# An input projection in rounds of wide and then narrow matmuls, and a first unit written out by hand

## The chip, the core and the metric

The kernel runs on one core of one Trainium2 chip. The time is device time in microseconds, from the launch's first to its last work, as the median of several runs. Engines in the views: PE is TensorE's matmuls, PEld its weight loads, DVE is VectorE, ACT is ScalarE, POOL is GpSimd, SP is the engine that issues most transfers. L343 is line 343 of the kernel.

## What is computed

Two layers of a mixer over 256 frames of width 2048, all in float32. In each layer the normalised input goes through one combined projection of 9248 columns; a pooling branch and a scanned state-space branch make 4096 columns of it, which an output projection brings back to 2048:

```python
for layer in range(DEPTH):
    h = rms_norm(x, pre_norm_w[layer])
    proj = jnp.einsum('bld,de->ble', h, w_in[layer])
    ...
    y_pool = pool_mixer(pool_u, pool_mix_w[layer], pool_scale[layer]) * jax.nn.silu(pool_gate)
    y_ssd = ssd_branch(ssd_z, ssd_xbc, ssd_dt, conv_w[layer], conv_b[layer], ...)
    mixed = jnp.concatenate([y_pool.astype(x.dtype), y_ssd.astype(x.dtype)], axis=-1)
    out = jnp.einsum('ble,ed->bld', mixed, w_out[layer])
    x = x + rms_norm(out, post_norm_w[layer])
```

## The kernel before

**Split operands.** Every matrix product is made from float32 numbers that are split into a high and a low part (type float32r): high weight times high and low input, and low weight times high input. The input `hs` holds, for each of its 16 slices of 128 rows, 256 columns of high parts and behind them 256 of low parts. A *wide* matmul takes a high weight block of 128x128 (`wh`) over all 512 columns, a *narrow* one the low block (`wl`) over the first 256. Both add to the same accumulator (`acc[m]`, 512 columns); `halves_sum` later adds its two halves with a ScalarE copy and a VectorE add, at a priority of 200 instructions ahead (`P_EVAC`).

**Units and halves.** Weights come in units of 512 rows by 512 columns (`raw`, three buffers, one transfer each on SP's queue; the first two units in pieces). Each unit is split in two halves of 256 rows by `emit_split`: ScalarE writes `wh`, VectorE subtracts and writes `wl`, five buffers each (`NW`). `run_ahead` emits the splits up to five halves past the one in use, with a priority of 15 instructions ahead (`P_SPLIT`), and fills free raw buffers.

**Chunks.** `chunk` makes 512 output columns: four accumulators of 128 columns, all four of the pool, over 16 slices, that is four units or 64 wide and 64 narrow matmuls. A layer has 18 such chunks: B, C and, for each of four groups, x, z, u and gate; behind each gate chunk stands a mix chunk of one unit (`pl` in place of `hs`). The first and the last unit go accumulator by accumulator through both halves, the middle ones half by half; `mm_m` does, for one accumulator and one half, wide, narrow, wide, narrow. `mid` is called twice in a unit and lets the background generators (scan, time steps, parameter loads) emit their next step. Chunk C also has 32 matmuls for the time-step columns in front of its first two units (`dt_unit`).

**Planner.** The program is traced in this order; a planner then orders each engine's instructions by priority and expected readiness, places buffers and sets the waits. `behind(...)` and `high_priority` bind or move single instructions.

**Start.** The first input piece comes in three transfers on ScalarE's queue, the first weight unit in three on SP's, the norm weights (`pre_rows`) on POOL's. `keep_busy` gives TensorE filler matmuls on the identity: 11 before the transpose of the norm weights, then the transposes of the first input slice (`piece`). In layer 0 the first unit goes slice by slice (`mm_k`, `by_k`, `piece_rest`), with the later slices' transposes and splits between.

Of the kernel before, what the change touches and what calls it, by code (L numbers as in the profile page):

```python
# [8 lines left out]
F32 = mybir.dt.float32  # L9
# [5 lines left out]
P = 128  # L15
# [26 lines left out]
def hybrid_kernel(ctx: ExitStack, tc, x, pre_norm_w, w_in, pool_mix_w, pool_scale, conv_w, conv_b,  # L42
# [15 lines left out]
    def t8():  # L58
        return work.tile([P, 8, SEQ], F32, name="t8", tag="t8", bufs=2)
# [86 lines left out]
    def emit_first(kk):  # L146
        if kk == 0:
            halves[0] = (wts.tile([P, 2, CW], F32R, name="wh", tag="wh", bufs=NW),
                         wts.tile([P, 2, CW], F32R, name="wl", tag="wl", bufs=NW))
            stream["split"] = 1  # L150
        wh, wl = halves[0]
        r = raws[0][:, kk]
        hi = nc.scalar.activation(out=wh[:, kk], in_=r, func=AF.Copy)
        lo = nc.vector.tensor_tensor(out=wl[:, kk], in0=r, in1=wh[:, kk].bitcast(F32), op=ALU.subtract)
        stream["last"] = (hi, lo)
# [48 lines left out]
    pre_rows = const.tile([DEPTH * NK, P], F32, name="pre_rows")  # L204
    load_pieces(x_in, emit_raw)
# [3 lines left out]
    nc.gpsimd.dma_start(out=pre_rows, in_=pre_norm_w.rearrange("l (a p) -> (l a) p", p=P))  # L209
# [38 lines left out]
    with tc.high_priority():  # L248
        idle = aux()
        filler = keep_busy(idle, 11)  # L250
# [5 lines left out]
        filler = pre_t  # L256
# [82 lines left out]
    def mm_m(acc, m, half, mov, k0, first, last):  # L339
        wh, wl = half  # L340
        cs = slice(m * P, (m + 1) * P)
        for kk in range(2):
            nc.tensor.matmul(acc[m], wh[:, kk, cs], mov[:, k0 + kk, :],  # L343
                             start=first and kk == 0, stop=False, skip_group_check=True)
            stream["mm"] = nc.tensor.matmul(acc[m][:, 0:SEQ], wl[:, kk, cs], mov[:, k0 + kk, 0:SEQ],  # L345
                                            start=False, stop=last and kk == 1, skip_group_check=True)

    def mm_k(acc, m, half, mov, k0, kk):
        wh, wl = half
        cs = slice(m * P, (m + 1) * P)  # L350
        nc.tensor.matmul(acc[m], wh[:, kk, cs], mov[:, k0 + kk, :],
                         start=k0 + kk == 0, stop=False, skip_group_check=True)
        stream["mm"] = nc.tensor.matmul(acc[m][:, 0:SEQ], wl[:, kk, cs], mov[:, k0 + kk, 0:SEQ],
                                        start=False, stop=False, skip_group_check=True)

    def chunk(mov, nk, pre_unit=None, mid_unit=None, by_k=None):
# [8 lines left out]

        for q in range(nq):
            if pre_unit is not None:
                pre_unit(q)
            if q == 0 and by_k is not None:
                hf = [next_half(False)]  # L370
                for h in range(2):
                    for kk in range(2):
                        if kk == 0 and h == 1:
                            hf.append(next_half(False))
                        for m in range(4):
                            mm_k(acc, m, hf[h], mov, 2 * h, kk)
                        if kk == 0 and h == 0:
                            by_k()
                        if h == 1:
                            mid(q, kk)  # L380
# [231 lines left out]
    later_k = []  # L612

    def piece(c):
        pts = [None, None]
        if c > 0:
            transpose_piece(c, range(NT), pts)
            return split_piece(0, c, hs, pts)
        with behind(filler):
            turned = transpose_piece(0, range(NT), pts, range(1))  # L620
        emit_first(0)
        with behind(pre_copy, *stream["last"]):
            first = split_piece(0, 0, hs, pts, range(1))
        turned = keep_busy(idle, 2, turned)
        with behind(turned):
            turned = transpose_piece(0, range(NT), pts, range(1, 2))
        with behind(*first):
            emit_first(1)
        with behind(*stream["last"]):
            second = split_piece(0, 0, hs, pts, range(1, 2))  # L630
        later_k.append((pts, second))
        return second

    def piece_rest():
        pts, second = later_k.pop()
        with behind(stream["mm"]):
            transpose_piece(0, range(NT), pts, range(2, 4))
        with behind(*second):
            rest = split_piece(0, 0, hs, pts, range(2, 4))
        with behind(*rest):  # L640
            run_ahead(2)
        return rest
# [3 lines left out]
    for l in range(DEPTH):  # L646
# [3 lines left out]
        gate = {0: piece(0)}  # L650
# [27 lines left out]
        def first_k(gate=gate):  # L678
            gate[0] = piece_rest()

        acc = chunk(hs, NK, None, first_mid, first_k if l == 0 else None)
# [29 lines left out]
        for g in range(NG):  # L711
# [18 lines left out]
            pl = work.tile([P, 4, CW], F32R, name="pl", tag="t8", bufs=2)  # L730
# [18 lines left out]
        pwb = work.tile([P, D_MODEL], F32, name="pwb", tag="t8", bufs=2)  # L749
# [132 lines left out]
```

## Time and profile before

| | us |
|---|---|
| median of 3 runs | 1284.42 (1284.25 to 1284.48) |
| the profiled execution | 1283.68 |
| its span, from the first to the last instruction | 1282.0 |
| TensorE busy in it | 1268.5 |
| VectorE, ScalarE, GpSimd busy | 919.9, 707.7, 194.1 |

A group of instructions by line has their count, the time in which any of them ran, the mean length of one in ns, and the idle time of the engine in front of them with what ended it. Ends of matmuls are modelled, and one matmul starts while the one before drains; where the pace of TensorE matters, starts are compared and not lengths. A row of the timeline has the start, the time until the last of the merged instructions ends, engine, line, operation and tiles, and in brackets idle time of that engine ahead of it.

### The profile page before, as it was taken

Reading aid. Unit: us, or ns where it says so; the run is one execution under the profiler, and the core shown is the slowest. Engines: PE = TensorE matmul, PEld = TensorE weight load, DVE = VectorE, ACT = ScalarE, POOL = GpSimd, SP = SyncE. Lnnn points to the kernel's source line nnn. Section 1 sums busy time; section 2 is a strip of 40 time slices with the busy share of each in tenths; the row PEclk is TensorE's granted clock in tenths of the full one; section 3 lists DMA queues with packets and bytes.
Section 4 is the critical chain, followed back from the end, with each engine's and each line's share of the span. In section 5 each row is a group of like instructions: output and inputs, shape, how many; then the busy total and the mean of one; then the engine's idle time right before and its main releaser. Section 6 shows DMA issues by size and latency. Waiting matters only on the chain.

```text
span 1282.0 us, 17907 instructions
## 1 busy us (share of the span) xinstructions
PE 1268.5 (99%) x6988; PEld 1087.5 (85%) x6988; DVE 919.9 (72%) x1297; ACT 707.7 (55%) x893; POOL 194.1 (15%) x245
## 2 busy tenths in 40 slices
PE   8999999999999999999999999999999999999997
PEld 7888888888888888888878888888888888888886
DVE  5898778868778794444478978778788788844454
ACT  6656556566566574344375566566565665644442
POOL 0111211212213220000002121122112122200000
PEclk9999999999999999999999999999999999999999
DMA  8555566465474676555564655555654655856552
GB/s 277 199 198 198 164 205 204 151 229 166 163 246 149 209 273 203 190 190 189 186 211 164 219 177 169 203 187 170 223 198 139 222 189 173 295 197 198 192 189 79
DMA packets 127244, 249.47 MB, mean 195 GB/s; under 512 B 9304, under 2 KB 10392, under 8 KB 125880
## 3 DMA queue, kind: packets, MB, share of 16 engines
q1 hardware_dynamic: 124808, 237.25, 55.9%
q0 software_dynamic: 1536, 10.57, 2.3%
q8 instruction: 54, 0.88, 0.3%
q10 hardware_dynamic: 816, 0.52, 0.1%
q14 instruction: 30, 0.25, 0.1%
HBM read 244.06 MB, written 4.26 MB: 194 GB/s over the span
## 4 chain that ended last, share of the span: by engine, by line
PE 97%; ACT 2%; DVE 1%; issue 0%; POOL 0%; POOLq 0%; ACTq 0%
PE acc L343 43%; PE acc L345 22%; PE acc L768 9%; PE acc L767 9%; PE acc L769 9%; PE aux L551 1%; PE aux L556 1%; PE aux L704 1%; PE aux L517 1%; ACT t L314 1%; PE aux L297 0%; ACT wh L138 0%; PE aux L245 0%; ACT hs L306 0%; PE aux L576 0%
## 5 line engine op out<-in xcount | busy, mean ns | idle before, releaser
L343 PE MATMUL acc<-hs,wh 128*128 128x512 f32 x2288 | 809.0, 398 | 1.0 <-DVE hs L307 1.0
L139 DVE TENSOR_TENSOR wl<-raw,wh 128x1024 fp32r<-128x1024 f32 x431 | 535.7, 1252 | 252.4 <-ACT wh L138 252.2
L138 ACT ACTIVATE wh<-raw 128x1024 fp32r<-128x1024 f32 x431 | 451.1, 1058 | 415.5 <-PE acc L343 222.9
L345 PE MATMUL acc<-hs,wl 128*128 128x256 f32 x2288 | 639.6, 280 | 0.0
L343 PEld LDWEIGHTS acc<-hs,wh 128*128 128x128 f32 x2288 | 429.2, 188 | 102.1 <-DVE hs L307 1.5
L345 PEld LDWEIGHTS acc<-hs,wl 128*128 128x128 f32 x2288 | 431.6, 189 | 1.2 <-DVE wl L139 0.2
L407 POOL TENSOR_TENSOR t<-t,rb 128x256 f32<-128x256 f32 x144 | 140.0, 981 | 405.6 <-DVE t L401 377.6
L400 ACT COPY t<-acc 128x256 f32<-128x256 f32 x176 | 63.0, 366 | 69.1 <-PE acc L345 69.0
L767 PE MATMUL acc<-wh,pm 128*128 128x512 f32 x256 | 99.7, 389 | 0.0
L767 PE MATMUL acc<-wh,ms 128*128 128x512 f32 x256 | 99.6, 389 | 0.0
L769 PE MATMUL acc<-wh,ms 128*128 128x512 f32 x256 | 99.6, 389 | 0.0
L768 PE MATMUL acc<-wl,ms 128*128 128x512 f32 x256 | 99.6, 389 | 0.0
L769 PE MATMUL acc<-wh,pm 128*128 128x512 f32 x256 | 99.6, 389 | 0.0
L768 PE MATMUL acc<-wl,pm 128*128 128x512 f32 x256 | 99.6, 389 | 0.0
L401 DVE TENSOR_TENSOR t<-acc,t 128x256 f32<-128x256 f32 x176 | 71.4, 416 | 14.7 <-ACT t L400 13.9
L420 DVE SCALAR_TENSOR_TENSOR t<-t,cols,t 128x256 f32<-128x256 f32 x144 | 70.8, 521 | 0.1
L767 PEld LDWEIGHTS acc<-wh,ms 128*128 128x128 f32 x256 | 48.1, 188 | 10.1
L767 PEld LDWEIGHTS acc<-wh,pm 128*128 128x128 f32 x256 | 48.1, 188 | 10.0
L769 PEld LDWEIGHTS acc<-wh,pm 128*128 128x128 f32 x256 | 48.1, 188 | 10.0
L769 PEld LDWEIGHTS acc<-wh,ms 128*128 128x128 f32 x256 | 48.1, 188 | 10.0
L768 PEld LDWEIGHTS acc<-wl,ms 128*128 128x128 f32 x256 | 48.1, 188 | 9.9
L768 PEld LDWEIGHTS acc<-wl,pm 128*128 128x128 f32 x256 | 48.1, 188 | 9.8
(158 smaller groups left out, 845.4 us busy)
## 6 DMA issues: line engine op xcount, KB each, us to landing
raw<-in_w_in_dram SPq DMA_DIRECT2D x142, 1024.0 KB, 5.1
raw<-in_w_out_dram SPq DMA_DIRECT2D x64, 1024.0 KB, 5.2
t<-acs POOLq DMA_DIRECT2D x8, 1024.0 KB, 5.1
raw<-in_pool_mix_w_dram SPq DMA_DIRECT2D x8, 1024.0 KB, 5.4
t<-in_x_dram SPq DMA_DIRECT2D x7, 512.0 KB, 9.5
pwb<-in_post_norm_w_dram POOLq DMA_DIRECT2D x2, 1024.0 KB, 7.3
x_mid<-t SPq DMA_DIRECT2D x8, 256.0 KB, 2.9
t<-x_mid SPq DMA_DIRECT2D x4, 512.0 KB, 8.8
```

The lines of the kernel that those rows point to most:

```text
L138: hi = nc.scalar.activation(out=wh, in_=r, func=AF.Copy)
L139: lo = nc.vector.tensor_tensor(out=wl, in0=r, in1=wh.bitcast(F32), op=ALU.subtract)
L314: nc.scalar.activation(out=junk, in_=xp[c][:, T], func=AF.Square, accum_out=ssq[:, T, c:c + 1])
L343: nc.tensor.matmul(acc[m], wh[:, kk, cs], mov[:, k0 + kk, :], start=first and kk == 0, stop=False, skip_group_check=True)
L345: stream["mm"] = nc.tensor.matmul(acc[m][:, 0:SEQ], wl[:, kk, cs], mov[:, k0 + kk, 0:SEQ], start=False, stop=last and kk == 1, skip_group_ ...
L400: nc.scalar.copy(out=t[0:n], in_=acc[0:n, SEQ:CW])
L401: nc.vector.tensor_tensor(out=t[0:n], in0=acc[0:n, 0:SEQ], in1=t[0:n], op=ALU.add)
L407: nc.gpsimd.tensor_tensor(out=dest[:, m], in0=t, in1=rb, op=ALU.mult)
L420: nc.vector.scalar_tensor_tensor(out=dst[:, m], in0=pad[:, m, j:j + SEQ], scalar=cw[:, j, ct:ct + 1], in1=dst[:, m], op0=ALU.mult, op1=ALU ...
L767: nc.tensor.matmul(oacc[T], ah, wh[:, kk], start=first and kk == 0, stop=False)
L768: nc.tensor.matmul(oacc[T], ah, wl[:, kk], start=False, stop=False)
L769: nc.tensor.matmul(oacc[T], al, wh[:, kk], start=False, stop=last and kk == 1)
```

## The change

Chunks other than B (those without a `mid_unit`, and C, which has a `pre_unit`) run in rounds of two units. A round asks for its four halves at once, then does 32 wide matmuls (first 16 accumulator by accumulator over the first two halves, then 16 half by half) and then 32 narrow ones (first 16 half by half, each half released after its eight, then 16 accumulator by accumulator over the last two halves). A mix chunk, of one unit, does 16 wide and then 16 narrow ones, both accumulator by accumulator. `mid` is called after each quarter of a round. In B's units `mm_m` now does two wide and then two narrow matmuls. The first unit of layer 0 is written out by hand in `first_unit`: for each slice, transposes, input split, weight split, four wide matmuls and four narrow ones, with an order between the splits. The norm weights are loaded on SP's queue in front of all else there; the first weight unit comes in four transfers instead of three; of the 11 fillers three stand before the transpose of the norm weights and eight behind it, and three (instead of two) behind the first slice's transposes. The buffers of tag t8 move to another pool.

```diff
-        return work.tile([P, 8, SEQ], F32, name="t8", tag="t8", bufs=2)
+        return wts.tile([P, 8, SEQ], F32, name="t8", tag="t8", bufs=2)
...
-            for a, b in (((0, 1), (1, 2), (2, 4)), ((0, 2), (2, 4)))[i]:
+            for a, b in (((0, 1), (1, 2), (2, 3), (3, 4)), ((0, 2), (2, 4)))[i]:
...
     pre_rows = const.tile([DEPTH * NK, P], F32, name="pre_rows")
+    nc.sync.dma_start(out=pre_rows, in_=pre_norm_w.rearrange("l (a p) -> (l a) p", p=P))
     load_pieces(x_in, emit_raw)
...
-    nc.gpsimd.dma_start(out=pre_rows, in_=pre_norm_w.rearrange("l (a p) -> (l a) p", p=P))
...
-        filler = keep_busy(idle, 11)
+        filler = keep_busy(idle, 3)
...
-        filler = pre_t
+        filler = keep_busy(idle, 8, pre_t)
...
+    def mm_wide(acc, m, half, mov, k0, first):
+        wh = half[0]
+        for kk in range(2):
+            stream["mm"] = nc.tensor.matmul(acc[m], wh[:, kk, m * P:(m + 1) * P], mov[:, k0 + kk, :],
+                                            start=first and kk == 0, stop=False, skip_group_check=True)
+
+    def mm_narrow(acc, m, half, mov, k0, last):
+        wl = half[1]
+        for kk in range(2):
+            stream["mm"] = nc.tensor.matmul(acc[m][:, 0:SEQ], wl[:, kk, m * P:(m + 1) * P], mov[:, k0 + kk, 0:SEQ],
+                                            start=False, stop=last and kk == 1, skip_group_check=True)
...
+        if mid_unit is None or pre_unit is not None:
+            per = min(nq, 2)
+            for s in range(nq // per):
+                for q in range(per):
+                    if pre_unit is not None:
+                        pre_unit(per * s + q)
+                run_ahead()
+                hf = [halves.pop(stream["use"] + i) for i in range(2 * per)]
+                last = s == nq // per - 1
+                k0 = 4 * per * s
+                for m in range(4):
+                    for h in range(2):
+                        mm_wide(acc, m, hf[h], mov, k0 + 2 * h, s == 0 and h == 0)
+                if per == 2:
+                    mid(2 * s, 0)
+                    for h in range(2, 4):
+                        for m in range(4):
+                            mm_wide(acc, m, hf[h], mov, k0 + 2 * h, False)
+                    mid(2 * s, 1)
+                    for h in range(2):
+                        for m in range(4):
+                            mm_narrow(acc, m, hf[h], mov, k0 + 2 * h, False)
+                        stream["use"] += 1
+                        run_ahead()
+                    mid(2 * s + 1, 0)
+                for m in range(4):
+                    for h in range(2 * per - 2, 2 * per):
+                        mm_narrow(acc, m, hf[h], mov, k0 + 2 * h, last and h == 2 * per - 1)
+                stream["use"] += 2
+                if per == 2:
+                    mid(2 * s + 1, 1)
+            return acc
...
+        turned = turn(range(1), filler)
+        keep_busy(idle, 3, turned)
+        x0 = split(0, pre_copy)
+        hi, lo = emit_first(0, (), (x0[1],))
+        wide(0, range(2))
+        turn(range(1, 2), stream["mm"])
+        wide(0, range(2, 4))
+        narrow(0)
+        x1 = split(1, x0[0], hi, lo)
+        w1 = emit_first(1, (x1[0],), (x1[1],))
+        wide(1, range(2))
+        turn(range(2, 4), stream["mm"])
+        wide(1, range(2, 4))
+        narrow(1)
+        x2 = split(2, w1[0], w1[1])
+        w2 = emit_first(2, (x2[0],), (x2[1],))
+        x3 = split(3, w2[0], w2[1])
+        w3 = emit_first(3, (x3[0],), (x3[1],))
+        wide(2, range(4))
+        stream["use"] = 2
+        with behind(*w3):
+            run_ahead(1)
+        return stream["last"], lambda: (narrow(2), wide(3, range(4)), narrow(3))
```

## Rows read from the trace of the kernel before

**Rows 1.** The page: busy us, share of the span and instructions of each engine.
```profile
PE 1268.5 (99%) x6988; PEld 1087.5 (85%) x6988; DVE 919.9 (72%) x1297; ACT 707.7 (55%) x893; POOL 194.1 (15%) x245
```
**Rows 2.** The page: the chain that ended last, by line.
```profile
PE acc L343 43%; PE acc L345 22%; PE acc L768 9%; PE acc L767 9%; PE acc L769 9%; PE aux L551 1%; PE aux L556 1%; PE aux L704 1%; PE aux L517 1%; ACT t L314 1%; PE aux L297 0%; ACT wh L138 0%; PE aux L245 0%; ACT hs L306 0%; PE aux L576 0%
```
**Rows 3.** The page: groups by line (count | busy us, mean ns | idle before).
```profile
L343 PE MATMUL acc<-hs,wh 128*128 128x512 f32 x2288 | 809.0, 398 | 1.0 <-DVE hs L307 1.0
L139 DVE TENSOR_TENSOR wl<-raw,wh 128x1024 fp32r<-128x1024 f32 x431 | 535.7, 1252 | 252.4 <-ACT wh L138 252.2
```
**Rows 4.** Timeline, PE: ends of two stretches of pairs (start us, us, what).
```profile
164.06 0.39 PE L343 MATMUL acc<-hs,wh 128*128 128x512 f32 x1
...
186.67 0.40 PE L343 MATMUL acc<-hs,wh 128*128 128x512 f32 x1
...
242.47 0.40 PE L343 MATMUL acc<-hs,wh 128*128 128x512 f32 x1
...
258.42 0.39 PE L343 MATMUL acc<-hs,wh 128*128 128x512 f32 x1
```
**Rows 5.** Timeline, PE: a run of wide matmuls in layer 0's output projection.
```profile
465.41 0.39 PE L767 MATMUL acc<-wh,ms 128*128 128x512 f32 x1
...
467.03 0.39 PE L768 MATMUL acc<-wl,ms 128*128 128x512 f32 x1
...
480.17 0.39 PE L769 MATMUL acc<-wh,ms 128*128 128x512 f32 x1
...
499.89 0.39 PE L769 MATMUL acc<-wh,pm 128*128 128x512 f32 x1
```
**Rows 6.** Timeline, all engines: a narrow matmul, the next weight load, the next matmul.
```profile
250.33 0.28 PE L345 MATMUL acc<-hs,wl 128*128 128x256 f32 x1
250.33 0.19 PEld L343 LDWEIGHTS acc<-hs,wh 128*128 128x128 f32 x1
250.44 0.39 PE L343 MATMUL acc<-hs,wh 128*128 128x512 f32 x1
```
**Rows 7.** Timeline, PE: in the first unit.
```profile
12.33 1.19 PE L351 MATMUL acc<-hs,wh 128*128 128x512 f32 x4 [0.25 <-ACT wh L138]
13.59 0.74 PE L353 MATMUL acc<-hs,wl 128*128 128x256 f32 x4
14.17 1.04 PE L297 MATMUL aux<-ident,t 128*128 128x128 f32 x8
```
**Rows 8.** Timelines of PE and DVE: accumulator 0, end of chunk u.
```profile
231.68 0.28 PE L345 MATMUL acc<-hs,wl 128*128 128x256 f32 x1
...
231.60 1.77 DVE L139 TENSOR_TENSOR wl<-raw,wh 128x1024 fp32r<-128x1024 f32 x1 [1.47 <-ACT wh L138]
233.29 0.95 DVE L401 TENSOR_TENSOR t<-acc,t 128x256 f32<-128x256 f32 x2
```
**Rows 9.** Timelines of PE and DVE: the same in x, z and gate.
```profile
182.31 0.28 PE L345 MATMUL acc<-hs,wl 128*128 128x256 f32 x1
...
183.38 0.42 DVE L401 TENSOR_TENSOR t<-acc,t 128x256 f32<-128x256 f32 x1
...
206.37 0.28 PE L345 MATMUL acc<-hs,wl 128*128 128x256 f32 x1
...
207.79 0.42 DVE L401 TENSOR_TENSOR t<-acc,t 128x256 f32<-128x256 f32 x1
...
254.49 0.28 PE L345 MATMUL acc<-hs,wl 128*128 128x256 f32 x1
...
256.20 0.88 DVE L401 TENSOR_TENSOR t<-acc,t 128x256 f32<-128x256 f32 x2
```
**Rows 10.** Start: timeline, then DMA issues (KB each, us from issue to landing).
```profile
1.36 0.69 POOL L209 DMA_DIRECT2D pre_rows<-in_pre_norm_w_dram  x1 [0.35 <-issue]
...
2.51 4.42 PE L245 MATMUL aux<-ident 128*128 128x128 f32 x22 [2.51 <-POOL ident masks.py:199]
...
pre_rows<-in_pre_norm_w_dram POOLq DMA_DIRECT2D x1, 16.0 KB, 4.6
```

More of the change, by code (lines that the diff above doesn't have):

```diff
@@ L337, in rstd_spread, with chunk @@
         return rb
-    def mm_m(acc, m, half, mov, k0, first, last):
[L340 to L356, printed above, removed]
+    def mm_wide(acc, m, half, mov, k0, first):
[8 more added lines that the diff above has]
+                                            start=False, stop=last and kk == 1, skip_group_check=True)
+    def mm_m(acc, m, half, mov, k0, first, last):
+        mm_wide(acc, m, half, mov, k0, first)
+        mm_narrow(acc, m, half, mov, k0, last)
+    def chunk(mov, nk, pre_unit=None, mid_unit=None, by_block=None):
         acc = [main() for _ in range(4)]
@@ L368, in chunk @@
                 pre_unit(q)
[L369 to L380, printed above, removed]
+            if q == 0 and by_block is not None:
+                by_block(acc)
+                step_bg()
+                step_bg()
             elif 0 < q < nq - 1:
@@ L610, in hybrid_kernel @@
     ssq = work.tile([P, NT, 4], F32, name="ssq", tag="ssq", bufs=2)
-    later_k = []
     def piece(c):
         pts = [None, None]
[L616 to L642, printed above, removed]
+        transpose_piece(c, range(NT), pts)
+        return split_piece(0, c, hs, pts)
+    def first_unit(acc):
+        pts = [None, None]
+        def turn(ks, after):
+            with behind(after):
+                return transpose_piece(0, range(NT), pts, ks)
+        def wide(kk, ms):
+            wh = halves[kk // 2][0]
+            for m in ms:
+                stream["mm"] = nc.tensor.matmul(acc[m], wh[:, kk % 2, m * P:(m + 1) * P], hs[:, kk, :],
+                                                start=kk == 0, stop=False, skip_group_check=True)
+        def narrow(kk):
+            wl = halves[kk // 2][1]
+            for m in range(4):
+                stream["mm"] = nc.tensor.matmul(acc[m][:, 0:SEQ], wl[:, kk % 2, m * P:(m + 1) * P], hs[:, kk, 0:SEQ],
+                                                start=False, stop=False, skip_group_check=True)
+        def split(kk, *after):
+            with behind(*after):
+                return split_piece(0, 0, hs, pts, range(kk, kk + 1))
+        turned = turn(range(1), filler)
[21 more added lines that the diff above has]
+        return stream["last"], lambda: (narrow(2), wide(3, range(4)), narrow(3))
@@ L649, in hybrid_kernel @@
         later = {}
-        gate = {0: piece(0)}
+        gate = {0: piece(0)} if l else {}
         stream["ahead"] = NW if l else 3
@@ L677, in first_mid, with by_block @@
                     later["wd"] = split_wdt(*later["wd"])
-        def first_k(gate=gate):
-            gate[0] = piece_rest()
-        acc = chunk(hs, NK, None, first_mid, first_k if l == 0 else None)
+        def by_block(acc, gate=gate, first_mid=first_mid):
+            gate[0], rest = first_unit(acc)
+            first_mid(0, 0)
+            rest()
+            first_mid(0, 1)
+        acc = chunk(hs, NK, None, first_mid, by_block if l == 0 else None)
         stream["ahead"] = NW
@@ L729, in hybrid_kernel @@
             evac(acc, u[:, :, PAD:PAD + SEQ], rb)
-            pl = work.tile([P, 4, CW], F32R, name="pl", tag="t8", bufs=2)
+            pl = wts.tile([P, 4, CW], F32R, name="pl", tag="t8", bufs=2)
             pool_window(g, u, pl)
@@ L748, in hybrid_kernel @@
         load_pieces(x_in if l == 0 else x_mid)
-        pwb = work.tile([P, D_MODEL], F32, name="pwb", tag="t8", bufs=2)
+        pwb = wts.tile([P, D_MODEL], F32, name="pwb", tag="t8", bufs=2)
         nc.gpsimd.dma_start(out=pwb, in_=post_norm_w[l].partition_broadcast(P))
```

21 lines of the change are left out of this document (13 added, 8 removed).

## The prediction

> **What bounds the kernel now.** Three views in this order. The page's busy times: TensorE is busy 1268.5 of 1282.0 us [rows 1], so all its idle time, start and end included, is 13.5 us. The chain of work that ended last: 65 points of it stand on lines 343 and 345, the wide and the narrow matmuls of the input projection, and 27 on the three lines of the output projection, which the change leaves alone [rows 2]. So nothing but PE's own pace in the input projection, or a new wait of PE, can move the time much. Then the groups by line: 2288 wide matmuls of line 343, 398 ns each by the modelled end, with 1.0 us of idle time ahead of all of them together [rows 3]. A modelled length has a tail in it that the next matmul overlaps, so it is the distance from start to start that prices a matmul, and for that I read the timeline.
>
> **The pace now.** Chunk x of group 1 runs wide, narrow, wide, narrow without another instruction between: 64 pairs from 164.06 to 186.67, 22.61 / 64 = 353 ns a pair. In the gate chunk of group 1, 46 pairs from 242.47 to 258.42, 15.95 / 46 = 347 ns [rows 4]. Both rhythms come back in every group. I take their mean, 350 ns, for all pairs that the change regroups. These are: per layer 17 chunks of 64 pairs (the first, B, keeps the old loop) and four mix chunks of 16, 1152; two layers, 2304 pairs.
>
> **The pace after.** *Wide.* A run of wide matmuls stands in the output projection, with the same sizes and types. Its first seven steps take 467.03 - 465.41 = 1.62 us, 231 ns each, and after that 87 steps take 499.89 - 480.17 = 19.72 us, 226.7 each [rows 5]. A run of 32 is then 7 x 231 + 25 x 226.7 = 7.28 us, 227.6 a matmul. Bounds 226.7 (settled at once) and 231.5 (never settled).
> *Narrow.* No long run stands in the trace. In the alternation the weight load of the next matmul begins with the narrow one, at 250.33, and the next matmul begins at 250.44, 0.11 to 0.12 later, though the load is drawn as 0.19 long [rows 6]. In a narrow run each step has the same load in front of it, so I take the same distance. The nearest row is the four narrow matmuls of the first unit: 13.59 to 14.17, 0.58 us, of which the first step is lengthened by the stall before it. The four wides at 12.33, also behind a stall, show by how much: (1.19 - 0.39) is 0.80 for three steps where two settled ones take 0.46, so 0.34 for the first, 0.11 too many. (0.58 - 0.11) / 4 = 117.5 ns [rows 7]. Bounds: 113 (the wide run's step scaled by half) and 120 (both steps lose the same 13 ns over their columns: 107 + 13). Eight transposes, each with a load of its own, keep 109 ns [rows 7], so a load alone does not forbid 113.
> A pair: 227.6 + 117.5 = 345 ns against 350. Gain 5 x 2304 = 11.5 us. Bounds: 226.7 + 113.3 = 340 gives 23 us; 231.5 + 120 = 351.5 costs 3.5 us.
> The page "TensorE: Matmul & The Clock Gate" of the Trainium skill (section Back-to-back issue gap) gives an isolated gap of N / 2.4 + 2.5 ns, 216 for 512 columns and 109 for 256; by it a pair of 325 would save 58 us. The settled run at 226.7 [rows 5] disagrees. The same page's LDWEIGHTS section puts a load at columns / 1.2, 107 ns, which speaks against any gain from narrow runs: no narrow matmul could go under its load. Transposes at 109 agree.
>
> **What the regrouping adds: the end of a chunk.** The four accumulators fill the pool "acc", so the next chunk's first wide matmul waits until accumulator 0 is read out: a ScalarE copy, then a VectorE add. Before, accumulator 0 is complete 12 pairs, 4.2 us, ahead of the chunk's end. After, only 12 narrow matmuls stand behind its last one: from that matmul's start to the next chunk's first is 13 x 117.5 = 1.53 us. What the read-out needs now, from the start of the last narrow on accumulator 0 to the end of the add: in u of group 1 from 231.68; the add waits behind a weight split (VectorE 231.60, 1.77 long) and ends near 233.71: 2.03 us [rows 8]. In x 182.31 to 183.80, 1.49; in z 206.37 to 208.21, 1.84; in the gate chunk 254.49 to 256.63, 2.14 [rows 9]. The shortest of these four, x, has 0.04 us to spare. If these delays stay, PE would idle 0, 0.3, 0.5 and 0.6 us, 1.4 us a group, 11 us for eight groups; with the mean of the four, 0.35, for the ten ends of C and of mix chunks that I did not read, 15 us, the upper bound for the forecast. The lower bound is 0 to 2: the add is placed with a priority of 200 instructions ahead, and the two low-half buffers that are freed in the narrow phase (2.9 and 1.9 us before the end, after 8 and 16 narrows) let VectorE do two splits of 1.25 us [rows 3] one behind the other and be done 0.4 us before the end, so that the add (0.42, [rows 9]) just fits. Where older VectorE work (the convolution, the decay of the scan) comes between, it doesn't. I take the middle, 8 us. Queued behind a waiting matmul is all of PE; nobody else is late by it.
>
> **Weights.** Four high halves are needed in a round, five buffers exist. High buffers 0 and 1 come free after 16 wides and the others by the end of the wides; the next round's second half is asked for 24 narrows (2.8 us) before it starts, one ScalarE copy, which I take as no longer than VectorE's 1.25 [rows 3]. Low halves have the whole wide phase, 7.3 us, for two splits. I cost these at nothing; if ScalarE is held up by more than 1.5 us there, wide matmuls wait on the copy of line 138, and the price is what is over. The t8 buffers change pools, addresses only. B chunk: two wides then two narrows instead of the alternation, nothing.
>
> **Start.** The load of the norm weights leaves POOL, where its issue of 0.69 us stood ahead of the identity; the fillers, now 2.51 to 6.93, can begin up to 0.7 us earlier [rows 10]. But only 6 filler matmuls (3 fillers) run before the transpose of those weights, and 16 behind it. On SP the load is issued about 0.5 us before POOL's; with its 4.6 us to landing [rows 10] it may arrive only at about 5.4, 16 fillers at 0.2 follow, and x is turned near 8.5 instead of just after 6.93. If it lands in 3 us, nothing is lost. Every other SP transfer is issued 0.4 to 0.8 us later (one transfer in front, one piece split in two); their users come late enough, the second x piece at 14.17 [rows 7]. In the first unit the wait at 12.33 (0.25) and the one before the narrows, which begin at 13.59, 0.46 after the fourth wide (12.33 + 0.80) instead of 0.23, may go [rows 7]. Start in sum: -0.5 us, bounds -1.5 and +2.
>
> **How the numbers follow.** -11.5 + 8 - 0.5 = -4.0 us. The profiled execution took 1283.68 (span 1282.0), so 1279.7; the median of the three runs is 0.74 above the profiled one, so **1280.4**. About 0.2%, 2.6 us, is what a measurement can tell from no change.
>
> **Rivals.** *Forecast, chance 0.50*: as above, 1273 to 1286; of it 0.37 faster, 0.10 same, 0.03 slower. *The accumulator wait outweighs the gain (0.24, of it 0.23 slower and 0.01 same)*: mechanism at the chunk end, price 0.5 us for each of 42 ends, 21 us, with a gain of 11.5 and 0.5 at the start: +9, 1293.4. It decides from a mean wait of 0.29 us (12 / 42). For it: 0.3 to 0.6 us in three of four chunk kinds read above; against: splits are then placed anew, and ScalarE is free at that point. *The pace does not change (0.11)*: 231 + 119 = 350, with waits of 1 to 6 us left: 1286 to 1290, near the edge between same and slower (0.07 same, 0.04 slower). For it: the first seven steps of a wide run, and the wides at 12.33, are no faster than the alternation's, and if the planner puts background matmuls between, a run starts anew each time, so that the change would not do what it says. *Narrow runs at 113 and hardly a wait (0.14, faster)*: 23 less 3, 1264. *The page's gap (0.01, faster)*: 1226.
>
> Faster by over 0.2%: 0.37 + 0.14 + 0.01 = 0.52; within: 0.10 + 0.07 + 0.01 from the accumulator case = 0.18; slower 0.30. The range reaches from 1266 to 1293, about one in ten left out on each side.
>
> **What would show it.** Right: wide starts 227 apart and narrow ones 117 within runs; pairs at 345; PE waits on the adds of `halves_sum` as the only new ones, 5 to 12 us in all. Wrong: wide steps of 231 and more deep in a run, narrow steps of 120 or more; a sum of waits over 12 us; waits on the split lines; the first wide matmul after 9.5 us.

## The result, and the profile after

| | before | after |
|---|---|---|
| median of 4 runs, us | 1284.34 | 1321.42 (1319.95 to 1322.51) |
| the profiled execution (its span), us | 1283.68 (1282.0) | 1322.51 (1320.8) |
| ratio of medians | | 1.0288 (1.0273 to 1.0303) |

The change makes the kernel 37.1 us slower. That lies outside the predicted range, on the side of the accumulator rival (1293.4), and well beyond it.

The page of after: the busy times, then the costliest groups of the two lines that are now the wide and the narrow matmuls, 347 and 353, and the first group of the output projection. They answer to [rows 1] and [rows 3].

```profile
PE 1280.0 (97%) x6990; PEld 1098.9 (83%) x6990; DVE 930.4 (70%) x1298; ACT 716.3 (54%) x902; POOL 213.1 (16%) x244
...
L347 PE MATMUL acc<-hs,wh 128*128 128x512 f32 x2288 | 555.9, 396 | 22.9 <-DVE t L430 21.9
...
L353 PE MATMUL acc<-hs,wl 128*128 128x256 f32 x2288 | 296.4, 284 | 0.0
L820 PE MATMUL acc<-wh,ms 128*128 128x512 f32 x256 | 99.9, 390 | 3.7 <-DVE t L430 3.7
```

Before, 1.0 us of idle time stood ahead of all wide matmuls together [rows 3]. Now it is 22.9 us, nearly all of it ended by VectorE's line 430, which is the add in `halves_sum`. The waits of PE in after, summed by what ended them, say the same (us in total, times, longest):

```profile
PE acc L347 <- DVE t L430: 25.5, 26, 3.1
PE acc L820 <- DVE t L430: 3.7, 2, 1.8
```

29.2 us in 28 waits, where before had none on that add. The chain that ended last stood on PE for 97% of the span. Now three other engines have 11% of it (by engine, before and after):

```profile
PE 97%; ACT 2%; DVE 1%; issue 0%; POOL 0%; POOLq 0%; ACTq 0%
...
PE 86%; DVE 6%; ACT 4%; issue 2%; POOL 1%; DMA 1%; ACTq 0%; DVEq 0%; SPq 0%; POOLq 0%
```

**Where the 39 us go.** That is the difference of the two profiled executions. I compared both traces by the distance from each matmul's start to the next one's, in us. Steps of at most 40 ns over the settled ones (226.7 wide, 120 narrow) are the pace: 5.9 less than before, 2.6 ns a pair, where 11.5 were forecast. Steps from a chunk's last narrow matmul, and stretches of background matmuls with the waits that stand directly behind them, are 35.8 more (20.7 and 15.1). Wide steps more than 130 ns too long are 4.4 more, most of them at half clock (below). Steps 40 to 130 ns too long are 5.6 more. Together that is +39.9; 1.0 of it is that TensorE starts its fillers that much earlier without finishing the start any earlier, which leaves the 39.0 by which the last matmul is later. The output projection is the same: from the first to the last matmul of each layer's it takes 348.7 us before and 348.9 after.

The first wide matmul starts at 8.6 us in both kernels, and the last matmul of chunk B at 34.9, so the rewritten start gives and costs nothing. Adding up what each chunk's end has in excess of a plain step, in after (in before it is zero for all but chunk B) gives 32.5 us:

| chunk that ends | excess at its end, us | sum |
|---|---|---|
| mix, before the next x (groups 0, 1, 2) | 1.53, 1.53, 0 in both layers | 6.1 |
| mix of group 3, before the output projection | 1.99, 2.00 | 4.0 |
| z of group 0 | 3.22, 2.76 | 6.0 |
| z of the other groups | 0.34 to 0.47, six times | 2.2 |
| u | six of 0.69 to 1.16, two of 0.13 | 6.7 |
| gate | 1.42 in group 3, else 0.06 to 0.17 | 3.4 |
| C | 0.80, 2.05 | 2.9 |
| x | 0.12 to 0.34 | 1.2 |

**The pace within rounds.** The timeline of PE in chunk x of group 1 in after (start, us until the last of the merged ones ends):

```profile
180.84 4.00 PE L353 MATMUL acc<-hs,wl 128*128 128x256 f32 x32
184.67 7.44 PE L347 MATMUL acc<-hs,wh 128*128 128x512 f32 x32
191.95 3.99 PE L353 MATMUL acc<-hs,wl 128*128 128x256 f32 x32
```

The 32 wide ones take 191.95 - 184.67 = 7.28 us, exactly the forecast. The 32 narrow ones take 184.67 - 180.84 = 3.83, 120 ns each, the pessimistic bound and not the 117.5 I took. A pair is then 227.5 + 119.7 = 347 ns: what the alternation already reached in the gate chunks [rows 4].

**A chunk's end.** Chunk u of group 1 in after, the timelines of PE, ACT and DVE:

```profile
241.44 3.99 PE L353 MATMUL acc<-hs,wl 128*128 128x256 f32 x32
246.40 1.20 PE L347 MATMUL acc<-hs,wh 128*128 128x512 f32 x4 [0.96 <-DVE t L430]
...
244.03 1.81 ACT L429 COPY t<-acc 128x256 f32<-128x256 f32 x4 [0.29 <-PE acc L353]
...
242.66 3.34 DVE L139 TENSOR_TENSOR wl<-raw,wh 128x1024 fp32r<-128x1024 f32 x2 [1.91 <-PE acc L353]
245.93 1.07 DVE L430 TENSOR_TENSOR t<-acc,t 128x256 f32<-128x256 f32 x3
```

ScalarE copies at once, at 244.03. VectorE cannot add before 245.93, because the two weight splits released by the narrow phase itself run ahead of it. TensorE is through its narrow matmuls by 245.4 and starts again at 246.40.

The mix chunk of group 1, timelines of PE, ACT, DVE and POOL:

```profile
273.00 2.08 PE L353 MATMUL acc<-pl,wl 128*128 128x256 f32 x16
274.91 0.60 PE L534 MATMUL aux<-t 128*128 128x256 f32 x2
276.90 2.35 PE L347 MATMUL acc<-hs,wh 128*128 128x512 f32 x9 [1.39 <-DVE t L430]
...
269.79 1.28 ACT L789 ACT_TABLE_LOAD   x1
274.13 1.06 ACT L789 ACTIVATE t<-t 128x1024 f32<-128x1024 f32 x1 [3.05 <-POOL t L436]
275.09 1.04 ACT L138 ACTIVATE wh<-raw 128x1024 fp32r<-128x1024 f32 x1
276.04 0.90 ACT L429 COPY t<-acc 128x256 f32<-128x256 f32 x3
...
270.15 3.35 DVE L139 TENSOR_TENSOR wl<-raw,wh 128x1024 fp32r<-128x1024 f32 x2
...
269.98 4.11 POOL L436 TENSOR_TENSOR t<-t,rb 128x256 f32<-128x256 f32 x3
```

Here ScalarE is late. The gate's Silu (line 789) stands ahead of the copies in its queue, and it waits 3.05 us for GpSimd's four products, which need the four gate accumulators. Before, these came out one by one from the last quarter of the gate chunk on and the Silu ran in the middle of the mix chunk; now they come out together at its end, and the mix chunk's own accumulators are complete before the Silu is done. The products are slow here too: the first, at 269.25, takes 0.74 us, the other three, beside two weight splits of VectorE, take 4.11.

### The profile page after: what moved, and what is told of

Same layout as the page of the kernel before. It is cut to its first block, busy times and chain, and to the rows that moved or that the text cites. A ratio compares the mean times of both kernels' runs of the same rounds, so it can differ in the third digit from the quotient of the medians.

```text
span 1320.8 us, 17891 instructions
## 1 busy us (share of the span) xinstructions
PE 1280.0 (97%) x6990; PEld 1098.9 (83%) x6990; DVE 930.4 (70%) x1298; ACT 716.3 (54%) x902; POOL 213.1 (16%) x244
## 4 chain that ended last, share of the span: by engine, by line
PE 86%; DVE 6%; ACT 4%; issue 2%; POOL 1%; DMA 1%; ACTq 0%; DVEq 0%; SPq 0%; POOLq 0%
PE acc L347 39%; PE acc L353 17%; PE acc L820 9%; PE acc L821 9%; PE acc L822 9%; DVE wl L139 3%; ACT wh L138 1%; POOL t L436 1%; PE aux L580 1%; DMA raw<-in_w_in_dram 1%; DVE t L430 1%; ACT t L319 1%; PE aux L585 1%; PE aux L757 1%; PE aux L250 0%
## 5 line engine op out<-in xcount | busy, mean ns | idle before, releaser
L139 DVE TENSOR_TENSOR wl<-raw,wh 128x1024 fp32r<-128x1024 f32 x430 | 550.7, 1305 | 245.9 <-ACT wh L138 168.8
L138 ACT ACTIVATE wh<-raw 128x1024 fp32r<-128x1024 f32 x430 | 446.0, 1056 | 449.6 <-PE acc L347 210.0
L347 PE MATMUL acc<-hs,wh 128*128 128x512 f32 x2288 | 555.9, 396 | 22.9 <-DVE t L430 21.9
L347 PEld LDWEIGHTS acc<-hs,wh 128*128 128x128 f32 x2288 | 423.5, 189 | 113.9 <-DVE t L430 29.4
L353 PEld LDWEIGHTS acc<-hs,wl 128*128 128x128 f32 x2288 | 290.1, 191 | 8.9
L353 PE MATMUL acc<-hs,wl 128*128 128x256 f32 x2288 | 296.4, 284 | 0.0
L436 POOL TENSOR_TENSOR t<-t,rb 128x256 f32<-128x256 f32 x144 | 160.5, 1143 | 387.2 <-DVE t L430 353.5
L430 DVE TENSOR_TENSOR t<-acc,t 128x256 f32<-128x256 f32 x176 | 63.1, 413 | 16.5 <-ACT t L429 16.3
L429 ACT COPY t<-acc 128x256 f32<-128x256 f32 x176 | 59.6, 374 | 26.3 <-PE acc L353 19.4
L449 DVE SCALAR_TENSOR_TENSOR t<-t,cols,t 128x256 f32<-128x256 f32 x144 | 65.7, 498 | 0.0
```

The source lines that it names most:

```text
L138: hi = nc.scalar.activation(out=wh, in_=r, func=AF.Copy)
L139: lo = nc.vector.tensor_tensor(out=wl, in0=r, in1=wh.bitcast(F32), op=ALU.subtract)
L347: stream["mm"] = nc.tensor.matmul(acc[m], wh[:, kk, m * P:(m + 1) * P], mov[:, k0 + kk, :], start=first and kk == 0, stop=False, skip_grou ...
L429: nc.scalar.copy(out=t[0:n], in_=acc[0:n, SEQ:CW])
L430: nc.vector.tensor_tensor(out=t[0:n], in0=acc[0:n, 0:SEQ], in1=t[0:n], op=ALU.add)
L436: nc.gpsimd.tensor_tensor(out=dest[:, m], in0=t, in1=rb, op=ALU.mult)
```

## Experiments

My theory, A in the expectations: the rounds lose the time, because all four accumulators of a chunk are finished together and the next chunk waits for their read-out. Against it stand that the rounds lose it in another way (pace, weight buffers, clock), and that the loss comes from the other parts of the change (the start, the moved buffers).

### Rounds alone, and start alone

The first run puts the round code, as in the diff, into the kernel before and leaves its start and the t8 buffers as they were. The second keeps the new start and the moved t8 buffers and takes the rounds out. (The new order in chunk B, two wide and then two narrow, is in neither.)

```diff
     def mm_m(acc, m, half, mov, k0, first, last):
-        mm_wide(acc, m, half, mov, k0, first)
-        mm_narrow(acc, m, half, mov, k0, last)
+        wh, wl = half
+        cs = slice(m * P, (m + 1) * P)
+        for kk in range(2):
+            nc.tensor.matmul(acc[m], wh[:, kk, cs], mov[:, k0 + kk, :],
+                             start=first and kk == 0, stop=False, skip_group_check=True)
+            stream["mm"] = nc.tensor.matmul(acc[m][:, 0:SEQ], wl[:, kk, cs], mov[:, k0 + kk, 0:SEQ],
+                                            start=False, stop=last and kk == 1, skip_group_check=True)
...
-        if mid_unit is None or pre_unit is not None:
-            per = min(nq, 2)
...
-            return acc
```

> The kernel before with the rounds alone: start, first unit and transfers as before. Theory A (the loss is PE's wait for the read-out of the accumulators at chunk ends: in the changed kernel 28 waits on the adds of halves_sum, 29 us of idle time) and rival B (the loss is in the pace of the regrouped matmuls themselves, narrow steps of 120 ns, runs broken by background work, a lower clock) both expect 1317 to 1323 us. Rival C (the loss comes from the hand-written start and the moved transfers, which shift everything behind them) expects 1284 to 1290.

Measured: 1322.18 against 1284.21, ratio 1.0293 (1.0278 to 1.0308). Its waits are those of after (line 446 is the add):

```profile
PE acc L342 <- DVE t L446: 26.1, 27, 2.9
PE acc L812 <- DVE t L446: 3.6, 2, 1.8
```

> The changed kernel without the rounds: every chunk in the old loop with wide and narrow matmuls alternating, the new start kept. A and B: 1283 to 1286 us, and the waits on the adds of halves_sum gone. C: 1310 or more.

Measured: 1278.69, ratio 0.9955 (0.994 to 0.997), below the 1283 to 1286 that I had expected. The rounds are the whole loss, and without them the rest of the change makes the kernel *faster* than before. But not at the start: its first wide matmul stands at 8.6 us as before, and up to chunk x of group 1 every chunk starts within 0.11 us of its time before. The last matmul starts 4.8 us earlier, and these come after that, in the mix, x and z chunks of groups 1 to 3.

### Where the 4.8 us come from: the t8 buffers

Kernel before with nothing but the tiles of tag t8 in the other pool:

```diff
     def t8():
-        return work.tile([P, 8, SEQ], F32, name="t8", tag="t8", bufs=2)
+        return wts.tile([P, 8, SEQ], F32, name="t8", tag="t8", bufs=2)
...
-            pl = work.tile([P, 4, CW], F32R, name="pl", tag="t8", bufs=2)
+            pl = wts.tile([P, 4, CW], F32R, name="pl", tag="t8", bufs=2)
...
-        pwb = work.tile([P, D_MODEL], F32, name="pwb", tag="t8", bufs=2)
+        pwb = wts.tile([P, D_MODEL], F32, name="pwb", tag="t8", bufs=2)
```

> The kernel before with one edit: the t8 buffers move to the other pool, so that they (the mix chunk's input among them) and what lies behind them have other addresses. e2 was 5.5 us faster than before, and its trace shows no gain at the start but a mix chunk in pairs of 346.7 ns instead of 352.8, a rhythm that the next chunks x and z keep. Theory D (the rhythm of alternating matmuls follows from where the operands lie): 1278 to 1281. Rival (it follows from the new order of instructions in the start and in unit 0): 1283 to 1286.

Measured: 1279.63 against 1284.37, ratio 0.9964 (0.9951 to 0.9977). Every engine runs the same instructions in the same order as before; only addresses differ, of the t8 buffers and of other tiles of their old pool. Of TensorE's operands in the projection `hs`, `wh` and `wl` stay where they were; the mix chunk's `pl` moves, from bytes 207680 and 215872 of each partition (its two buffers) to 169088 and 177280. First and 16th wide matmul of the mix chunk of group 1, in before:

```profile
258.76 0.39 PE L343 MATMUL acc<-pl,wh 128*128 128x512 f32 x1
...
264.06 0.40 PE L343 MATMUL acc<-pl,wh 128*128 128x512 f32 x1
```

and with t8 moved:

```profile
258.25 0.39 PE L343 MATMUL acc<-pl,wh 128*128 128x512 f32 x1
...
263.45 0.40 PE L343 MATMUL acc<-pl,wh 128*128 128x512 f32 x1
```

5.30 / 15 = 353 ns a pair against 5.20 / 15 = 347. So the two rhythms of [rows 4] are two states of the same instruction stream. The one that the mix chunk falls into is kept by the x chunk behind it (353.3 before, 346.7 moved, mean of its 64 pairs) and by part of z (351.1 and 347.4, without the pairs that a background matmul splits). A third place, bytes 195200 and 203392, by pools for t4 and t8 of their own:

```diff
-    work = ctx.enter_context(tc.tile_pool(name="work", bufs=1))
+    p4, mid8 = (ctx.enter_context(tc.tile_pool(name=n, bufs=1)) for n in ("p4", "mid8")); work = ctx.enter_context(tc.tile_pool(name="work", bufs=1))
...
-        return work.tile([P, 8, SEQ], F32, name="t8", tag="t8", bufs=2)
+        return mid8.tile([P, 8, SEQ], F32, name="t8", tag="t8", bufs=2)
...
-        return work.tile([P, 4, PAD + SEQ], F32, name="t4", tag="t4", bufs=6)
+        return p4.tile([P, 4, PAD + SEQ], F32, name="t4", tag="t4", bufs=6)
```

> The kernel before with the t8 buffers at a third place in each partition: byte 195200 (before: 207680, e5: 169088); weights, input and mixer output lie where they lay. Theory D says that the mix chunk's rhythm follows from the place of its input: either 346.7 ns and 1278 to 1281, or 352.8 and 1283 to 1286, a number between the two in the mix chunks would speak against two rhythms. If the place doesn't matter and something else in e5 did it: 1283 to 1286.

Measured: 1279.81, ratio 0.9965 (0.9952 to 0.9978), pairs again 347 ns in the mix chunks of groups 0 to 2. But the place alone does not decide. The mix chunk of group 3, whose `pl` is the other one of the two buffers, runs at 353 ns in both layers of this run. With nothing but t8 moved it runs at 353 in layer 0 and at 347 in layer 1 (first and 16th wide matmul):

```profile
457.81 0.40 PE L343 MATMUL acc<-pl,wh 128*128 128x512 f32 x1
...
463.11 0.40 PE L343 MATMUL acc<-pl,wh 128*128 128x512 f32 x1
...
1089.95 0.39 PE L343 MATMUL acc<-pl,wh 128*128 128x512 f32 x1
...
1095.15 0.39 PE L343 MATMUL acc<-pl,wh 128*128 128x512 f32 x1
```

In the second run, with t8 at that same place, it runs at 347 in both. Both edits also shift other tiles of the old pool (t1 and t2 by 16384 bytes), so these runs do not tell the place of `pl` from theirs. What they show is that moving buffers, without any regrouping, is worth the 4.7 us; what makes a rhythm slow stays open.

### More accumulators

If the wait is for accumulators, a fifth one should hide much of it, and a sixth more. The bank comes from the pool of the background matmuls (three and two left of four). The same edit in the kernel before shows what the smaller pool costs by itself.

```diff
-    ps_main = ctx.enter_context(tc.tile_pool(name="ps_main", bufs=4, space=PSUM))
-    ps_aux = ctx.enter_context(tc.tile_pool(name="ps_aux", bufs=4, space=PSUM))
+    ps_main = ctx.enter_context(tc.tile_pool(name="ps_main", bufs=5, space=PSUM))
+    ps_aux = ctx.enter_context(tc.tile_pool(name="ps_aux", bufs=3, space=PSUM))
```

> The changed kernel with five accumulator buffers instead of four (three instead of four for the other PSUM tiles). A chunk's first accumulator then needs no read-out, its second needs that of the last chunk's first, 0.9 us later than now, and so on: 1.4 us more slack at each end. A: the waits of 1.1 to 1.5 us at the ends of u and gate chunks go, those of 2.1 at mix ends shrink to about 0.7 and of 4 at the end of z in group 0 to 2.6: 9 us left of 34, so 1293 to 1299 us. B: 1318 to 1322, the pace isn't touched.

> Control: the kernel before with five accumulators and three other PSUM tiles. It has no wait at chunk ends to lose. A and B: 1283 to 1287 us; if it is faster by more than 2 us, e3's gain isn't all the chunk ends'; if slower, three other PSUM tiles cost something in e3 too.

Measured: after with five 1306.7, ratio to before 1.0173 (1.0156 to 1.019); before with five 1283.31, ratio 0.9994 (0.9984 to 1.0003). So 14.7 us of the loss go with one more accumulator, less than I had expected (1293 to 1299). Its waits:

```profile
PE acc L347 <- DVE t L430: 15.6, 11, 3.2
PE acc L820 <- DVE t L430: 2.7, 2, 1.4
PE aux L580 <- DVE t L570: 1.9, 6, 0.7
```

11 waits on the adds instead of 26: those at the ends of u are gone. At the end of z of group 0 TensorE only gets four wide matmuls further, into the fifth accumulator, and then waits as long as before:

```profile
109.77 0.64 PE L353 MATMUL acc<-hs,wl 128*128 128x256 f32 x4
110.25 1.09 PE L347 MATMUL acc<-hs,wh 128*128 128x512 f32 x4
114.57 6.64 PE L347 MATMUL acc<-hs,wh 128*128 128x512 f32 x28 [3.23 <-DVE t L430]
```

The same with six and two:

> The changed kernel with six accumulator buffers and two other PSUM tiles. Two of a chunk's four accumulators then need no read-out of the last chunk, the third needs it 1.9 us later than now. With five (e3) 18 us of waits on the adds were left of 29. A: nearly all go except at the end of z in group 0, 1283 to 1292 us; what is then left over 1278.7 (e2) isn't the read-out's. B: over 1300.

> Control for e10: the kernel before with six accumulators and two other PSUM tiles. A: 1283 to 1288, two tiles for scan and transposes may cost a little. If it is slower by more than 5 us, e10 has to be read beside it.

Measured: after with six 1299.23, ratio 1.0116 (1.0099 to 1.0133), a miss, since I had expected 1283 to 1292; before with six 1284.07, ratio 1.0002 (0.9993 to 1.0012). Waits of after with six:

```profile
PE aux L585 <- DVE t L589: 9.0, 8, 1.5
PE aux L580 <- DVE t L570: 4.2, 7, 1.6
PE acc L347 <- DVE t L430: 3.6, 6, 1.6
```

The adds are down to 3.6 us. New waits stand at the scan's background matmuls. Line 585 needs a third background buffer where there are now two, and waits until VectorE's line 589 has read one; line 580 waits for its operand from line 570, as it did for 1.9 us with five. The kernel before does with two without loss, so it takes rounds and two buffers together; I did not separate them further. This run also shows the most that rounds could bring. Against the second run (1278.69), which has everything but the rounds, its steps of plain pace (as defined above) sum up to 1.3 us less, in 1279. All the rest is loss.

### Half a chunk in rounds

The first two units of a chunk in a round, the last two and the mix chunks by alternation. A chunk then ends as before, accumulator by accumulator with 4 us to spare.

```diff
-            for s in range(nq // per):
+            for s in range(1 if per == 2 else 0):
...
-            return acc
...
-        for q in range(nq):
+        for q in range(2 if nq > 1 and (mid_unit is None or pre_unit is not None) else 0, nq):
```

> The changed kernel with rounds in a chunk's first half alone; its second half, and mix chunks, alternate as before, so that accumulator 0 is complete 4.2 us ahead of the end again. A (read-out at the chunk's end): no waits over 0.3 us there, 1277 to 1283. B (the regrouped pace, broken runs or the clock cost the time): half of the loss stays, 1296 to 1304.

Measured: 1293.31 against 1284.37, ratio 1.0072 (1.0057 to 1.0087). I had expected under 1283: a miss, and the waits say why for about half of it. They are 6.8 us on the adds, at the *start* of chunks, of the 14.6 us that lie between this run and the second one (1278.69); the rest, in longer steps, I did not take apart. Chunk z of group 2, PE:

```profile
288.89 0.28 PE L362 MATMUL acc<-hs,wl 128*128 128x256 f32 x1
289.01 2.89 PE L347 MATMUL acc<-hs,wh 128*128 128x512 f32 x12
292.65 4.60 PE L347 MATMUL acc<-hs,wh 128*128 128x512 f32 x19 [0.75 <-DVE t L434]
```

Twelve wide matmuls, 2.7 us, and the round wants the fourth accumulator, which was finished last, at 289.01. The alternation asks for it after 12 pairs, 4.2 us. So grouping shortens the slack on both sides of the read-out. (At 1293.3 it is still 13 us better than a full round with five accumulators.)

### The late Silu of the mix chunk

First attempt: the Silu is written after the four `halves_sum` of the mix chunk instead of before it.

```diff
-            nc.scalar.activation(out=gs, in_=gs, func=AF.Silu)
 
             acc = chunk(pl, 4)
+            sums_m = [halves_sum(acc[m]) for m in range(4)]
+            nc.scalar.activation(out=gs, in_=gs, func=AF.Silu)
```

> The changed kernel with one instruction moved: the gate's Silu comes behind the read-out of the mix chunk's accumulators instead of ahead of it. In the changed kernel ScalarE stands at that Silu, which waits for GpSimd's four products, with the copies of the accumulators behind it in its queue, and PE waits 2.1 us at the ends of mix chunks. A with that cause: these waits (six of 2.1, and two of 2.0 ahead of the output projection) go, 1305 to 1309. If they come from VectorE's splits instead: 1319 to 1323.

Measured: 1323.66, ratio 1.0308 (1.0292 to 1.0324). The planner put the Silu ahead of the copies all the same (Silu 272.36, copies from 274.27), so this run says nothing about the theory. The second attempt binds it behind the last copy:

```diff
-            nc.scalar.copy(out=t[0:n], in_=acc[0:n, SEQ:CW])
+            stream["copy"] = nc.scalar.copy(out=t[0:n], in_=acc[0:n, SEQ:CW])
...
+            sums_m = [halves_sum(acc[m]) for m in range(4)]
+            with behind(stream["copy"]):
+                nc.scalar.activation(out=gs, in_=gs, func=AF.Silu)
```

> e7 again, with the Silu bound behind the last copy of the mix accumulators in ScalarE's queue: in e7 the planner put it ahead of the copies all the same, so that e7 tested nothing. If ScalarE's standing at the Silu causes the waits at the ends of mix chunks (2.1 us, six of them, and two of 2.0 ahead of the output projection): 1305 to 1311, and these waits under 0.6 us. If not: 1319 to 1324.

Measured: 1312.53 against 1284.17, ratio 1.0216 (1.0201 to 1.0231), 9 us better than after and 1.5 more than the 1311 that I had put as the most. Timelines of PE and ACT at the same place as above:

```profile
269.82 2.08 PE L353 MATMUL acc<-pl,wl 128*128 128x256 f32 x16
271.74 5.50 PE L347 MATMUL acc<-hs,wh 128*128 128x512 f32 x23
...
271.80 0.91 ACT L429 COPY t<-acc 128x256 f32<-128x256 f32 x3
272.73 1.28 ACT L793 ACT_TABLE_LOAD   x1
274.02 1.06 ACT L793 ACTIVATE t<-t 128x1024 f32<-128x1024 f32 x1
```

The wait is gone at the mix ends of groups 0 and 1, four ends and not the six that I had counted (group 2 had none). That the copies stood behind the Silu was the cause there. At the output projection 1.6 us of 2.0 stay.

### Narrow matmuls accumulator by accumulator

The last 32 narrow matmuls of a chunk go through all four halves for one accumulator after the other, so that the first is complete 24 narrow steps, 2.9 us, before the end instead of 12.

```diff
-                    for h in range(2):
-                        for m in range(4):
-                            mm_narrow(acc, m, hf[h], mov, k0 + 2 * h, False)
-                        stream["use"] += 1
-                        run_ahead()
-                    mid(2 * s + 1, 0)
+                    if not last:
...
-                    for h in range(2 * per - 2, 2 * per):
+                    for h in range(0 if last else 2 * per - 2, 2 * per):
```

> The changed kernel with all 32 narrow matmuls of a chunk's last round in the order of the accumulators (not only the last 16), so that accumulator 0 is complete 24 narrow matmuls, 2.9 us, ahead of the end instead of 1.4. The splits that were asked for in this phase come later, at the next chunk's start. A: the waits at the ends of u, z and gate chunks (1.1 to 4 us, 18 us in all) shrink by 1.4 us each at most, the mix ends keep theirs: 1306 to 1312, unless the later splits make new waits for the first wide matmuls, which would show on line 138. B: 1319 to 1323.

Measured: 1313.8, ratio 1.023 (1.0213 to 1.0247), 7.6 us better than after. The ends of u, x and gate have no excess any more (for gate of group 3 it was 1.42). A mix end of groups 0 and 1 still has 0.9, the ends of z up to 0.9, C in layer 1 1.5, and the start of the output projection 2.4 instead of 2.0. That is half of what a fifth bank gives, without the bank, a little less than the 1306 to 1312 that I had expected, and it still loses to the alternation.

## Why the prediction was wrong, point by point

**What bounds the kernel: right.** Only TensorE's pace in the input projection and new waits of it moved the time. The output projection takes the same to 0.2 us (348.7 and 348.9).

**The wide run: right to 0.01 us** (7.28 for 32).

**The narrow run: the term was mis-sized.** Not 117.5 but 120 ns. The four narrow matmuls of [rows 7] behind a stall, with a correction taken from four others, were a weak base; the bound "both steps lose the same 13 ns", 120, was the truth. With it a pair is 347, and against the mean of 350 the gain is 6 to 7 us instead of 11.5 (5.9 by the steps). In this term the truth lay midway between the forecast and the third rival, "the pace does not change".

**The mean of the two rhythms: the step that hid the real comparison.** I took 350 ns as the price of the alternation. But the fast rhythm of [rows 4], 347, and the slow one, 353, are not properties of chunk kinds. In most mix chunks and the x chunks behind them the slow one goes away when buffers move, without any regrouping. I costed that move at nothing ("addresses only"), and it is worth 4.7 us by itself. Rounds with the old place (1322.18) and with the new one (1321.42) differ by 0.8 only. So most of what grouping gains over before was to be had by the move, and beyond it grouping gains 1.3 us.

**The accumulator wait: right place and right mechanism, wrong size. This is the step that turned the sign.** I put down 8 us with an upper bound of 15; it measured 29.2 us of idle time, 32.5 in excess steps, and in the profiled execution drags another 4 us of half clock behind it. Three parts failed:

- *Chunk ends that I did not read.* I gave the ten ends of C and mix chunks the mean of four others, 3.5 us in all. They cost 13. The mix end has a ScalarE step in its way that no other end has, the Silu, and the regrouping itself made it late, because it gathers the gate's four read-outs at one point. Binding it behind the copies took 6.9 of the 13 away and made the kernel 9 us faster.
- *One group read for all.* The z chunk of group 1 was read, and forecast at 0.3 us; it measured 0.34 to 0.47 there and in groups 2 and 3. In group 0 the scan's instructions lie at that end: the copies come at 112.33 behind four other ScalarE instructions and the adds at 114.44 behind two splits that take 2.88 us together. It cost 3 us in each layer.
- *The splits in front of the add.* I wrote that the two splits take 1.25 us each and that the add then just fits. At u they did run ahead of the add, but took 3.34 us for two, 1.67 each. GpSimd ran two products of the scan (lines 600 and 601) beside them; its second took 1.61 us, where in before the product of the same size took 0.74. At the gate end of group 1, with GpSimd idle, two splits took 2.36. One split of 1.77 us already stood in [rows 8]. The page "SBUF — State Buffer" of the Trainium skill (section SBUF: two separate sides) says that a VectorE operation with two SBUF inputs and a GpSimd operation that reads SBUF hold a shared port against each other. The lengthening on both engines, 1.67 instead of 1.18 us and 1.61 instead of 0.74, agrees.

The gate ends, forecast at 0.6 us, were over-priced: six of eight have 0.06 to 0.17.

**The accumulator rival, 0.24,** had the mechanism and the sign. Its price of 0.5 us for each of 42 ends was my guess from the same four delays. Measured, 32.5 us over 42 ends is 0.77, with a gain of 6 instead of 11.5 set against it.

**Weights at nothing: right for TensorE's waits** (no wide or narrow matmul of a round waits on a split), but not for VectorE's queue, as above.

**Start: within its bounds.** -0.5 was forecast, 0 measured: the fillers do begin 1.0 us earlier, but the first wide matmul stands at 8.6 in both kernels.

**What the forecast did not have at all:** the clock. The windows of PE after the z end of group 0 (us; busy us and matmuls; granted clock; DMA):

```profile
111.00:113.00 2.00, 0.82 (x8) 1.00 0.01 4
113.00:115.00 2.00, 0.10 (x1) 0.76 0.18 38
115.00:117.00 2.00, 2.00 (x5) 0.50 1.02 373
117.00:119.00 2.00, 2.00 (x6) 0.50 0.52 157
119.00:121.00 2.00, 2.00 (x7) 0.54 1.00 357
121.00:123.00 2.00, 2.00 (x10) 1.00 0.32 124
```

TensorE had been idle for 3.09 us up to 114.90. The clock fell to its lower level, 1.2 GHz, within that wait and was back at 2.4 GHz before 121, and 12 wide steps took some 427 ns each instead of 227, 2.4 us more. In layer 1 it happened again, with 7 such steps. So in this execution the wait of 3.1 us cost some 5.5. The length of a wait does not settle it, though. With five accumulators TensorE waited 3.23 us at the same place and the clock stayed at 1.00; in the first attempt on the Silu it fell after a wait of 1.84 us ahead of the output projection (PE, one window of each run):

```profile
115.00:117.00 2.00, 2.00 (x11) 1.00 1.00 374
...
484.00:486.00 2.00, 2.00 (x6) 0.50 1.03 357
```

Nor is the clock the loss: the run of after with a mean granted clock of 0.999 (0.994 in the profiled one) still took 1319.95 us.

**The best version.** The kernel after without the rounds (1278.69, ratio to before 0.9955) and the kernel before with the t8 buffers moved (1279.63, 0.9964) are both faster than before and than after; their intervals overlap.

## What to carry to other kernels

Before regrouping matmuls for pace, ask whether the existing order already reaches that pace somewhere in the trace; if it does, find out what separates its slow stretches from its fast ones: here moving buffers gave most of the gain. Grouping by kind makes all accumulators finish together: count the slack of their read-out at both ends, in TensorE steps, against the longest queue on the engines that read them, and read every kind of chunk end and every group, since the sum is carried by the few worst. More buffers cure only the waits that are shorter than the work they let in.

## What the runs showed of the hardware that I had not expected

- An alternation of 512- and 256-column matmuls has two steady rhythms, 346.7 and 353.3 ns a pair, with the same instructions and the same granted clock (1.00). The slow one has a period of three pairs (steps of 236, 113, 233, 117, 241 and 120 ns), the fast one steps of 230 and 116 to 117. Moving the t8 buffers took the mix chunks of groups 0 to 2 from the slow to the fast one, and the x chunk behind each stays in it, though its own operands had not moved. The mix chunk of group 3 ran in either with its operand at one and the same place.
- A run of narrow matmuls settles at 120 ns a step, though eight transposes, each with its own weight load, run at 109 [rows 7].
- A split of VectorE and a product of GpSimd that overlap both take longer: 1.67 instead of 1.18 us, and 1.61 instead of 0.74.
- TensorE's granted clock fell to 0.50 after a wait of 1.84 us in one run and stayed at 1.00 after one of 3.23 us in another.
